# Places in SBUF: weight tiles and the activations that meet them begin at multiples of 256 bytes

## The chip, the cores and the metric

The kernel runs on one core of a Trainium2 chip. The metric is the device time of one execution in microseconds (us): the median over several runs. A profiled execution gives one further time and the trace that the views below are taken from.

## What is computed

One layer of a streaming encoder, on 512 tokens of 1024 channels, all in float32. Cut to what matters:

```python
h = rms_norm(x, norm_mix_pre)
(a_q, a_k, a_v, f_q, f_k, f_v, f_g, c_u, s_x, s_b, s_c) = split(h @ w_in)
ya = diff_attention(a_q, a_k, a_v, lam)            # 4 heads, rms norm behind it
yf = forgetting_attention(f_q, f_k, f_v, log_f)    # 8 heads
yc = silu(layer_norm(dwconv31(glu(c_u))))
ys = s_b * dwconv3(s_c * s_x)
gates = sigmoid(h @ w_gate + b_gate)               # 4 x 1024 columns
mixed = sum_n(gates[n] * (y[n] @ w_branch[n])) @ w_out
x = x + rms_norm(mixed, norm_mix_post)
hx = rms_norm(x, norm_x_pre); m = rms_norm(mem, norm_mem)
x = x + rms_norm(cross_attention(hx @ w_xq, m @ w_xkv) @ w_xo, norm_x_post)
hf = rms_norm(x, norm_ffn_pre)
u_g, u_v = split(dwconv3(hf @ w_up))               # 2 x 2816 columns
x = x + rms_norm((silu(u_g) * u_v) @ w_down, norm_ffn_post)
```

## The kernel before

**Three products for one.** Every large matrix product is made of three matmuls in the type float32r. Each operand is held as a high part and a low part (what the high part leaves over): hth and htl for the activations, wh and wl for the weights, and so on. `mm3` (L195) issues high x high, high x low and low x high into the same PSUM bank, through `matmul` (L187), so nearly all matmuls have L188 as their line. A matmul has two operands in SBUF: the **stationary** one, 128 columns, loaded into TensorE ahead of it, and the **moving** one, up to 512 columns, streamed through. `channel_major` (L201) makes an output with channels on partitions: for each of 8 blocks of 128 input channels a 128 x 128 piece of the weights is stationary and 512 tokens of ht move; that is 24 matmuls for one weight block. In `v_jobs`, `mix_out_jobs`, `vx_jobs`, `cross_out_jobs` and `down_jobs` (L1240) it is the other way round: 128 tokens of the activation are stationary and 512 columns of the weights move.

**Weights.** All weights come in 180 blocks of 512 KB (four of 520 KB). `load_raw` (L128) issues the DMA from SP into one of two raw tiles wr; `split_weights` (L136) makes wh by a copy on ScalarE (L148) and wl by a subtraction on VectorE (L149). wh and wl have four buffers each, which come round by turns (the pool gives out a buffer that has been released). A tile of them has WB = 1040 float32 elements, 4160 bytes to a partition; most blocks fill 4096 of these, the block of the forget values (`vf_jobs`, 2 x 520 columns) all. `run_blocks` (L161) goes through one list of jobs (`all_jobs`, L1283): it fetches two blocks ahead, then runs a block's body.

**Order.** A scheduler of the language orders each engine's instructions at build time, but for the first stretch of the kernel, which is written out by hand (`keep`, L264). Small tasks (attention steps, convolution taps, norms) are put between the blocks by `Background` (L44) with estimated costs. In order of time: the first columns of w_in with the norm of x (to 35 us), the convolution and short-convolution columns, the gates and branches in turn with the two attentions (to some 590 us), the output projection, the cross attention (640 to 740 us), the up-projection (44 blocks, to 973 us) and the down-projection (22 blocks, to the end). The up-projection has two outputs of 128 x 512 for each of its 22 pairs of blocks; the down-projection adds up in all eight PSUM banks at once: for a block, each of four token tiles has two halves of 512 columns with three matmuls each, and two banks of one tag stand for a token tile, so that six matmuls in a row name the same PSUM tag.

**Where tiles stand.** Pools give tiles their places in SBUF, in the order in which tiles are first asked for, one behind another. The pool "g" (L86) lies at the low end and holds ident, ht, the mask, wr, wh, wl and small tiles; the pools m2, res, work and ffn follow it upward; the pools m1, xm, mix and xp are taken from the upper end. All pieces within a tile that matmuls read begin at multiples of 256 bytes from the tile's start, but in the block of the forget values, where half of them begin 32 further. These are the places (bytes from the start of a partition) of the built programs, taken modulo 256:

| tile | met by | before | after |
|---|---|---|---|
| hth, htl (h, hx, hf) | w, wa | 160, 160 | 0, 0 |
| wh, wl: buffers 1 to 4, in the order of their first use | ht, y8, mix, mt, ox, act | 32, 224, 160, 96 | 0, 0, 0, 0 |
| wa (first columns, high and low) | ht | 160 | 160 |
| y8 (branch outputs) | w | 224 | 0 |
| mixh, mixl | w | 96 | 0 |
| mth, mtl; later oxh, oxl | w | 96 | 0 |
| kx / xq | each other | 96 / 224 | 0 / 128 |
| vx / pth, ptl of the cross attention | each other | 224 / 96 | 0 / 0 |
| acth, actl | w | 224 | 0 |
| qk; v and pth, ptl of the attentions | themselves; each other | 160; 32 | 160; 32 |
| wr (raw weights; DMA, ScalarE, VectorE) | no matmul | 160, 224 | 128, 192 |

wh and wl of one block always stand at the same place modulo 256.

Of the kernel before, what the change touches and what calls it, by code (L numbers as in the profile page):

```python
# [16 lines left out]
F32 = mybir.dt.float32  # L17
F32R = mybir.dt.float32r
# [6 lines left out]
P = 128  # L25
S = 512
D = 1024
NT = S // P
NK = D // P
# [4 lines left out]
NF = DFF // P  # L34
EPS = 1e-6
WB = 2 * 520
BIG = -float(2.0 ** 100)
LAMBDA_INIT = 0.8 - 0.6 * math.exp(-0.3 * 0)

# [41 lines left out]
def hybrid_layer(ctx: ExitStack, tc: tile.TileContext, a: dict, out: bass.AP):  # L81
# [4 lines left out]
    gp = ctx.enter_context(tc.tile_pool(name="g", bufs=1))  # L86
# [7 lines left out]
    def bank(tag=None):  # L94
        if tag is None:
            turn_of.n += 1
            tag = "av" if turn_of.shared and turn_of.n % 2 else "mm"
        return psum.tile([P, 512], F32, tag=tag, name=f"ps_{tag}", bufs=2)
# [14 lines left out]
    G.memset(nhalf, -0.5)  # L113


    def split(ps, hi, lo, scale=None):

        if scale is None:
            A.copy(hi, ps)  # L119
            V.tensor_tensor(lo, ps, hi.bitcast(F32), ALU.subtract)  # L120
        else:
            A.activation(hi, ps, AF.Copy if isinstance(scale, float) else AF.Identity, scale=scale)
            V.scalar_tensor_tensor(lo, ps, scale, hi.bitcast(F32), ALU.mult, ALU.subtract)
# [4 lines left out]
    def load_raw(src, shape, order=same):  # L128

        n = int(math.prod(shape[1:]))  # L130
        raw = gp.tile([P, WB], F32, tag="wr", name="wr", bufs=2)
        t = raw[:, :n]
# [3 lines left out]
    def split_weights(raw, shape, low=V, order=same):  # L136

        n = int(math.prod(shape[1:]))
        hi = gp.tile([P, WB], F32R, tag="wh", name="wh", bufs=4)
        lo = gp.tile([P, WB], F32R, tag="wl", name="wl", bufs=4)  # L140
        names = "k c" if len(shape) == 3 else "c"
        form = f"p ({names}) -> p {names}"

        def view(t):
            t = t[:, :n]
            return t.rearrange(form, k=shape[1]) if len(shape) == 3 else t

        order(A.copy(hi[:, :n], raw[:, :n]))  # L148
        low.tensor_tensor(lo[:, :n], raw[:, :n], hi[:, :n].bitcast(F32), ALU.subtract)  # L149
        return view(hi), view(lo)  # L150

    def load_weights(src, shape, low=V, order=same):
        return split_weights(*load_raw(src, shape), low, order)
# [77 lines left out]
    def to_channels(y_t, act, t):  # L231

        sl = slice(t * P, (t + 1) * P)
        for half in range(2):
            ps = bank("tr")
            ks = slice(half * 4, half * 4 + 4)
            for k in range(4):
                transpose(ps[:, k * P:(k + 1) * P], y_t[:, (half * 4 + k) * P:(half * 4 + k + 1) * P])
            split(ps.rearrange("p (k c) -> p k c", k=4), act[0][:, ks, sl], act[1][:, ks, sl])

    def new_ht():
        return (gp.tile([P, NK, S], F32R, tag="hth", name="hth"),
                gp.tile([P, NK, S], F32R, tag="htl", name="htl"))


    ht = new_ht()
    tc.swap_default_side()
    m1 = tc.tile_pool(name="m1", bufs=1)
# [10 lines left out]
    G.memset(mask_a, 0.0)  # L259
    G.memset(mask_a[0:HD, S - HD:S], BIG)  # L260

# [38 lines left out]
    for i, plan in enumerate(plans):  # L300
        r_t = m1p.tile([P, P], F32, tag="fbias" if i == 2 else "ck", name=f"rows{i}", bufs=2)
        n = 0
# [92 lines left out]
    for p in range(3):  # L395
        first_half(1, p, w_a[1], glu)
    casts = []
    w_g = [split_weights(*raw, V, lambda ins: casts.append(keep(ins))) for raw in raw_g]


# [9 lines left out]
    def pc(name, j=0, n=1):  # L410
        i, base = where[name]
        return par[i][:, base + j:base + j + n]
# [7 lines left out]
            par.append(t)  # L420

    def scaled(name, n, factor):
        t = gp.tile([P, n], F32, name=f"s_{name}")
        V.tensor_scalar(t, pc(name, 0, n), factor, None, ALU.mult)
        return t

# [2 lines left out]
    def finish_init():  # L429
        to_columns()  # L430
        half["glu"] = scaled("b_glu", 8, 0.5)
        half["gate"] = scaled("b_gate", 32, 0.5)
        half["ln_g"] = scaled("ln_g", 4, 0.5)
        half["ln_b"] = scaled("ln_b", 4, 0.5)
        half["dn"] = scaled("dn", 1, 1.0 - LAMBDA_INIT)

    lam = gp.tile([P, 1], F32, name="lam")
    bfg = gp.tile([P, 8], F32, name="bfg")


    def y8(dtype=F32R):
# [275 lines left out]


    crows = dram.tile([8, S], F32, name="crows")
    cq = gp.tile([P, NT, 8], F32, name="cq")  # L720

    def vf_jobs(dst):

# [79 lines left out]
    def f_task(p, qk, v):  # L803
# [10 lines left out]
        for step in range(6):  # L814
# [17 lines left out]
            if step < 4:  # L832
# [3 lines left out]
                for j in range(2):  # L836
# [5 lines left out]
                    G.affine_select(out=bias[:, w - P:w], in_=bias[:, w - P:w], pattern=[[-1, P]],  # L842
                                    compare_op=ALU.is_ge, fill=BIG, base=0, channel_multiplier=1)
                    ps = bank("sc")
# [94 lines left out]
    ns = SimpleNamespace()  # L939

    def new_pool(name, right):
        if right:
            tc.swap_default_side()
        pool = tc.tile_pool(name=name, bufs=1, reuse_waits="tile")
        handle = pool.__enter__()
        if right:
            tc.swap_default_side()
        return pool, handle

    def close(pool):  # L950
        pool.__exit__(None, None, None)

    def stage(tag, name):
        return ns.xm.tile([P, D], F32, tag=tag, name=name)

    def open_last_branch():
        close(m1)
        ns.xm_, ns.xm = new_pool("xm", True)
        ns.mt = (ns.xm.tile([P, NK, MEM], F32R, tag="mth", name="mth"),
                 ns.xm.tile([P, NK, MEM], F32R, tag="mtl", name="mtl"))  # L960
        ns.kx = (ns.xm.tile([P, 4, MEM], F32R, name="kxh"), ns.xm.tile([P, 4, MEM], F32R, name="kxl"))
        ns.gain = stage("s0", "g_mem")
        G.dma_start(ns.gain, a["norm_mem"][0].partition_broadcast(P))
        bg.add(mem_task(), "mem")
        ns.mix_, ns.mixp = new_pool("mix", True)
        ns.mix = (ns.mixp.tile([P, NK, S], F32R, name="mixh"), ns.mixp.tile([P, NK, S], F32R, name="mixl"))

    def mem_task():
        for t in range(2):
            m_t = stage("s1", "m_t")  # L970
            G.dma_start(m_t, mem_d[t * P:(t + 1) * P, :])
            y_t = normed(ns.xm, m_t, [ns.gain], stage("s2", "mn"))
            yield 1.3, 8.0
            to_channels(y_t, ns.mt, t)
            yield 1.2, 0.0
# [25 lines left out]
    def last_branch_jobs():  # L1001
        yield then(open_last_branch)
        yield from gate_blocks(1, "f", lambda m: split(acc[m], ns.mix[0][:, m], ns.mix[1][:, m], 0.5))
# [26 lines left out]
    def open_mix_out():  # L1030
        close(m2)
        ns.res_, resp = new_pool("res", False)
        ns.out = [resp.tile([P, D], F32, name=f"res{t}") for t in range(NT)]
        ns.work_, ns.work = new_pool("work", False)
        ns.vx = (ns.work.tile([P, 2, BR], F32R, name="vxh"), ns.work.tile([P, 2, BR], F32R, name="vxl"))
        ns.post, ns.pre = stage("s0", "g_post"), stage("s1", "g_pre")
        G.dma_start(ns.post, a["norm_mix_post"][0].partition_broadcast(P))
        G.dma_start(ns.pre, a["norm_x_pre"][0].partition_broadcast(P))
        ns.hx = new_ht()
        ns.x = {}  # L1040
        load_x(0)
        load_x(1)
# [116 lines left out]
    def open_cross_out():  # L1159
        ns.ox = (ns.xm.tile([P, 4, S], F32R, tag="mth", name="oxh"),  # L1160
                 ns.xm.tile([P, 4, S], F32R, tag="mtl", name="oxl"))
        ns.post, ns.pre = stage("s0", "g_post2"), stage("s1", "g_pre2")
        G.dma_start(ns.post, a["norm_x_post"][0].partition_broadcast(P))
        G.dma_start(ns.pre, a["norm_ffn_pre"][0].partition_broadcast(P))
        ns.hf = new_ht()
# [162 lines left out]
```

## Time and profile before

| | |
|---|---|
| median of 3 runs | 1102.9 us (1102.79 to 1107.03) |
| the profiled execution's own time | 1103.45 us |
| its span, first to last instruction | 1101.7 us |
| TensorE (PE) busy | 1088.4 us, 5445 matmuls |
| VectorE (DVE), ScalarE (ACT) busy | 695.2 and 463.4 us |
| mean granted TensorE clock | 0.998 of full speed |
| DMA | 109.29 MB, 99 GB/s |

The page of the profile gives busy times by engine, then the chain that ended last (from the last instruction back, at each step to what released it), then groups of equal instructions: line, engine, operation, output<-inputs, shapes, count, then busy us and mean ns of one, then the idle time before them with what ended it. PE stands for matmuls, PEld for the loads of stationary operands. Matmuls are pipelined, and the printed time of one contains the wait behind its predecessor: 5445 matmuls of mostly 390 ns would be far more than the span. Their starts follow each other at 230 ns or so, and it is the starts that carry time. The chain's own view in order of time merges neighbours of one group: start, duration, engine, output, line, count.

### The profile page before, as it was taken

Reading aid. Unit: us, or ns where it says so; the run is one execution under the profiler, and the core shown is the slowest. Engines: PE = TensorE matmul, PEld = TensorE weight load, DVE = VectorE, ACT = ScalarE, POOL = GpSimd, SP = SyncE. Lnnn points to the kernel's source line nnn. Section 1 sums busy time; section 2 is a strip of 40 time slices with the busy share of each in tenths; the row PEclk is TensorE's granted clock in tenths of the full one; section 3 lists DMA queues with packets and bytes.
Section 4 is the critical chain, followed back from the end, with each engine's and each line's share of the span. In section 5 each row is a group of like instructions: output and inputs, shape, how many; then the busy total and the mean of one; then the engine's idle time right before and its main releaser. Section 6 shows DMA issues by size and latency. Waiting matters only on the chain.

```text
span 1101.7 us, 14173 instructions
## 1 busy us (share of the span) xinstructions
PE 1088.4 (99%) x5445; PEld 912.7 (83%) x5445; DVE 695.2 (63%) x1128; ACT 463.4 (42%) x783; POOL 100.6 (9%) x186
## 2 busy tenths in 40 slices
PE   8999999999999999999999999999999999999997
PEld 7888888888888988888888899788888888888886
DVE  6899986466666367757563486668666666642224
ACT  5322222467464365554432455545444444431111
POOL 4000001000101033323010110120000000000001
PEclk9999999999999999999999999999999999999999
DMA  6433433332122243333252263133333333323222
GB/s 198 115 96 82 96 96 98 94 96 77 58 86 69 79 114 96 96 96 115 86 180 94 80 188 101 56 97 115 96 96 96 96 96 96 95 96 96 96 77 77
DMA packets 145849, 109.29 MB, mean 99 GB/s; under 512 B 3648, under 2 KB 133293, under 8 KB 145782
## 3 DMA queue, kind: packets, MB, share of 16 engines
q1 hardware_dynamic: 143221, 99.85, 30.4%
q0 software_dynamic: 2560, 8.54, 2.7%
q8 instruction: 43, 0.70, 0.3%
q14 instruction: 25, 0.20, 0.1%
HBM read 106.27 MB, written 2.11 MB: 98 GB/s over the span
## 4 chain that ended last, share of the span: by engine, by line
PE 94%; DMA 2%; DVE 1%; ACT 1%; issue 1%; POOL 0%; POOLq 0%; DVEq 0%; SPq 0%; ACTq 0%
PE ps_mm L188 49%; PE ps_av L188 30%; PE ps_sc L188 8%; PE ps_tr L192 3%; PE ps_tr L188 3%; DVE wl L149 1%; DMA wr<-in_w_xo 1%; ACT wh L148 1%; PE ps_mm L369 1%; PE ps_av L369 1%; DMA wr<-in_w_xkv 0%; DMA wr<-in_w_xq 0%; DMA xs<-in_x 0%; POOL st_r L218 0%; ACT hth L119 0%
## 5 line engine op out<-in xcount | busy, mean ns | idle before, releaser
L149 DVE TENSOR_TENSOR wl<-wr,wh 128x1024 fp32r<-128x1024 f32 (+1 forms) x180 | 222.1, 1235 | 216.0 <-ACT wh L148 215.3
L148 ACT CAST wh<-wr 128x1024 fp32r<-128x1024 f32 (+1 forms) x180 | 188.5, 1049 | 340.5 <-PE ps_mm L188 127.6
L188 PE MATMUL ps_mm<-hth,wh 128*128 128x512 f32 (+1 forms) x608 | 233.7, 385 | 0.4 <-ACT hth L119 0.2
L188 PE MATMUL ps_mm<-hth,wl 128*128 128x512 f32 (+1 forms) x608 | 232.5, 382 | 0.0
L188 PE MATMUL ps_mm<-htl,wh 128*128 128x512 f32 (+1 forms) x608 | 232.3, 382 | 0.2 <-DVE htl L120 0.2
L188 PEld LDWEIGHTS ps_mm<-hth,wh 128*128 128x128 f32 x608 | 114.4, 188 | 22.2 <-ACT hth L119 0.5
L188 PEld LDWEIGHTS ps_mm<-hth,wl 128*128 128x128 f32 x608 | 114.3, 188 | 22.3
L188 PEld LDWEIGHTS ps_mm<-htl,wh 128*128 128x128 f32 x608 | 114.4, 188 | 21.6 <-DVE htl L120 0.5
L188 PE MATMUL ps_av<-hth,wh 128*128 128x512 f32 (+1 forms) x336 | 127.2, 379 | 0.2
L188 PE MATMUL ps_av<-htl,wh 128*128 128x512 f32 (+1 forms) x336 | 126.9, 378 | 0.0
L188 PE MATMUL ps_av<-hth,wl 128*128 128x512 f32 (+1 forms) x336 | 126.9, 378 | 0.0
L517 DVE SCALAR_TENSOR_TENSOR y<-y,par,y 128x499 f32<-128x499 f32 (+28 forms) x120 | 82.4, 731 | 0.2
L188 PEld LDWEIGHTS ps_av<-hth,wh 128*128 128x128 f32 x336 | 63.2, 188 | 13.1 <-DVE e L864 0.5
L188 PEld LDWEIGHTS ps_av<-hth,wl 128*128 128x128 f32 x336 | 63.2, 188 | 12.6
L188 PEld LDWEIGHTS ps_av<-htl,wh 128*128 128x128 f32 x336 | 63.2, 188 | 12.4
L188 PE MATMUL ps_mm<-y,wh 128*128 128x512 f32 x192 | 61.5, 397 | 0.0
L215 POOL TENSOR_SCALAR st_m<-pm,pm 128x1 f32<-128x1 f32 x12 | 4.6, 387 | 483.5 <-ACT junk L1269 357.5
L188 PEld LDWEIGHTS ps_mm<-y,wh 128*128 128x128 f32 x192 | 35.4, 188 | 7.3
L188 PE MATMUL ps_mm<-y,wl 128*128 128x512 f32 x96 | 37.9, 395 | 0.0
L119 ACT CAST acth<-c 128x512 fp32r<-128x512 f32 x22 | 13.6, 620 | 55.8 <-DVE c L1216 55.8
L119 ACT CAST pth<-ps_tr 128x512 fp32r<-128x512 f32 (+3 forms) x56 | 23.6, 450 | 28.8 <-PE ps_tr L192 26.1
L120 DVE TENSOR_TENSOR ptl<-ps_tr,pth 128x512 fp32r<-128x512 f32 (+3 forms) x56 | 28.0, 513 | 10.6 <-ACT pth L119 10.3
(373 smaller groups left out, 1893.8 us busy)
## 6 DMA issues: line engine op xcount, KB each, us to landing
wr<-in_w_up SPq DMA_DIRECT2D x44, 512.0 KB
wr<-in_w_in SPq DMA_DIRECT2D x38, 512.0 KB
wr<-in_w_gate SPq DMA_DIRECT2D x32, 512.0 KB
wr<-in_w_down SPq DMA_DIRECT2D x22, 512.0 KB
wr<-in_w_branch SPq DMA_DIRECT2D x16, 512.0 KB
wr<-in_w_out SPq DMA_DIRECT2D x8, 512.0 KB
wr<-in_w_xkv SPq DMA_DIRECT2D x8, 512.0 KB
wr<-in_w_in SPq DMA_DIRECT2D x4, 520.0 KB
```

Source lines behind the costliest of these rows:

```text
L119: A.copy(hi, ps)
L120: V.tensor_tensor(lo, ps, hi.bitcast(F32), ALU.subtract)
L148: order(A.copy(hi[:, :n], raw[:, :n]))
L149: low.tensor_tensor(lo[:, :n], raw[:, :n], hi[:, :n].bitcast(F32), ALU.subtract)
L188: PE.matmul(ps, lhs, rhs, start=start, stop=stop)
L192: PE.transpose(ps, x, ident[:n, :n])
L215: G.tensor_scalar(m, parts[0], parts[1], EPS, ALU.add, ALU.add)
L369: keep(PE.matmul(banks[c][:, :S // 2], w[p == 1][:, k, c * P:(c + 1) * P], ht[p == 2][:, i * 4 + k, :S // 2], start=(i, p, k) == (0, 0, 0) ...
L517: V.scalar_tensor_tensor(dst[:, s:], src[:, :S - s], pc("conv_dw", k * 4 + j), dst[:, s:], ALU.mult, ALU.add)
```

## The change

No instruction is added or taken away; tiles are taken in another order, and some space is left between them.

- `small` and `ht_tiles` take the small tiles lam, bfg and s_dn, and then the first hth and htl, ahead of the others, so that ht begins at a multiple of LINE = 256. `new_ht` (L241) hands out these two first.
- The eight weight tiles are taken at once, wh and wl in turn. Behind the first stand s_b_gate, s_b_glu and s_ln_g (176 bytes, rounded up by the pool to 192); behind each of the next six a gap of 192 bytes; behind the last cq, s_ln_b and a gap of 160. Each tile has a tag of its own; `weights_tile` counts the uses and goes round the four in a fixed order.
- A gap of 96 bytes in the pool xm, behind kx, sets mt, kx, mix and what follows in the upper pools.
- All else moves by what lies below it (the table above).

```diff
+LINE = 256
...
+    small = {n: gp.tile([P, k], F32, name=n) for n, k in (("lam", 1), ("bfg", 8), ("s_dn", 1))}
+    ht_tiles = [gp.tile([P, NK, S], F32R, tag=n, name=n) for n in ("hth", "htl")]
+    w_tiles, w_used = {}, {"wh": 0, "wl": 0}
+
+    def space(pool, name, n):
+
+        if n:
+            pool.tile([P, n // 4], F32, name=name)
+
+    for i in range(8):
+        n = ("wh", "wl")[i % 2]
+        w_tiles[n, i // 2] = gp.tile([P, WB], F32R, tag=f"{n}{i // 2}", name=n)
+        if i == 0:
+            small.update((n, gp.tile([P, k], F32, name=n)) for n, k in (("s_b_gate", 32), ("s_b_glu", 8), ("s_ln_g", 4)))
+        elif i < 7:
+            space(gp, f"gap{i}", -4 * WB % LINE)
+    small.update((n, gp.tile([P, k], F32, name=n)) for n, k in (("cq", NT * 8), ("s_ln_b", 4)))
+    space(gp, "gap7", 160)
+
+    def weights_tile(kind):
+
+        i = w_used[kind]
+        w_used[kind] += 1
+        return w_tiles.pop((kind, i), None) or gp.tile([P, WB], F32R, tag=f"{kind}{i % 4}", name=kind)
...
-        hi = gp.tile([P, WB], F32R, tag="wh", name="wh", bufs=4)
-        lo = gp.tile([P, WB], F32R, tag="wl", name="wl", bufs=4)
+        hi, lo = weights_tile("wh"), weights_tile("wl")
...
     def new_ht():
+        if ht_tiles:
+            return ht_tiles.pop(0), ht_tiles.pop(0)
...
-        t = gp.tile([P, n], F32, name=f"s_{name}")
+        t = small[f"s_{name}"]
...
-    lam = gp.tile([P, 1], F32, name="lam")
-    bfg = gp.tile([P, 8], F32, name="bfg")
+    lam, bfg = small["lam"], small["bfg"]
...
-    cq = gp.tile([P, NT, 8], F32, name="cq")
+    cq = small["cq"].rearrange("p (t h) -> p t h", t=NT)
...
+        space(ns.xm, "gap8", 96)
```

## The prediction

> **What bounds the kernel.** I read the page first, then the chain of work that ended last, then the starts of TensorE's instructions one by one.
>
> ```profile
> span 1101.7 us, 14173 instructions
> ...
> PE 1088.4 (99%) x5445; PEld 912.7 (83%) x5445; DVE 695.2 (63%) x1128; ACT 463.4 (42%) x783; POOL 100.6 (9%) x186
> ...
> PE 94%; DMA 2%; DVE 1%; ACT 1%; issue 1%; POOL 0%; POOLq 0%; DVEq 0%; SPq 0%; ACTq 0%
> PE ps_mm L188 49%; PE ps_av L188 30%; PE ps_sc L188 8%; PE ps_tr L192 3%; PE ps_tr L188 3%; DVE wl L149 1%; DMA wr<-in_w_xo 1%; ACT wh L148 1%; PE ps_mm L369 1%; PE ps_av L369 1%; DMA wr<-in_w_xkv 0%; DMA wr<-in_w_xq 0%; DMA xs<-in_x 0%; POOL st_r L218 0%; ACT hth L119 0%
> ...
> L148 ACT CAST wh<-wr 128x1024 fp32r<-128x1024 f32 (+1 forms) x180 | 188.5, 1049 | 340.5 <-PE ps_mm L188 127.6
> ```
>
> The chain is 94% TensorE, nearly all of it line 188. The last line says who waits for whom: ScalarE, which makes the high parts of the weights, sits idle because TensorE hasn't yet given a buffer back. So the time is the number of matmuls times the distance between their starts. (The printed 385 ns of a matmul is no price: matmuls overlap. I take start to start.) 3871 of the 5445 rows are 512 columns wide; their starts take up 899.3 us, 232.3 ns each. Long waits are few: behind the first 20 us only six, all between 641 and 740 us, hold TensorE by over 0.3 us beyond a matmul's own time, 4.3 us together.
>
> **A natural experiment in the trace of before.** The up-projection is the cleanest stretch: blocks of 24 equal matmuls, no waits. The chain there, columns start us, us, what:
>
> ```profile
> 851.53 5.50 PE ps_mm L188 x24
> 857.03 5.60 PE ps_av L188 x24
> 862.62 5.46 PE ps_mm L188 x24
> 868.09 5.58 PE ps_av L188 x24
> ```
>
> Same instruction, same shape, same granted clock of 1.00, yet four durations that come round every four blocks: that is the rotation of the four wh/wl buffers. A tile of 4160 bytes shifts the next one's place by 64 modulo 256. The table of places ahead of this section gives the rest: the moving hth and htl stand at 160, and the four stationary blocks above stand at 96, 224, 160 and 32. I call **distance** the place of the stationary operand less that of the moving one, modulo 256: here 192, 64, 0 and 128. Distance 0 is the shortest block. I laid the program's 5440 matmuls beside the trace's rows, in order, and grouped the 512-wide ones (intervals over 250 ns left out of the means):
>
> - distance 0: 932, mean 228.6 ns; in the steady part of a block 226.7
> - distance 64: 1068, mean 233.2 (steady 231 and 236 in turn, or 233)
> - distance 128: 804, mean 232.4 (a pattern between 228 and 241)
> - distance 192: 1066, mean 229.6 (226, 229, 232 in turn)
>
> Is it the distance, or the buffer? The down-projection has the sides exchanged: w moves, act (at 224) is stationary, so that another buffer, the one at 224, is at distance 0. The chain there:
>
> ```profile
> 989.99 1.40 PE ps_mm L188 x6
> 991.38 1.37 PE ps_av L188 x6
> 992.75 1.36 PE ps_sc L188 x6
> 994.11 1.36 PE ps_tr L188 x6
> 995.47 1.40 PE ps_mm L188 x6
> 996.87 1.40 PE ps_av L188 x6
> 998.27 1.40 PE ps_sc L188 x6
> 999.67 1.40 PE ps_tr L188 x6
> ```
>
> The first four rows are the buffer at 224: after one row of settling 1.36 us for 6, or 226.7 ns. The next four are the buffer at 160, distance 64: 1.40, or 233.3. In the up-projection these two were the other way round. So the distance decides, not the buffer, the PSUM bank or the time.
>
> The Trainium skill ("SBUF — State Buffer", sections "SBUF: two separate sides" and "A bandwidth-pool intuition that's wrong") says that TensorE's SBUF ports never wait on anyone and that LDWEIGHTS has a second, independent read port; by it places cost nothing, the sum is 0 and the time stays 1102.9. The trace doesn't agree: 5.46 against 5.60 us for the same 24 matmuls.
>
> **The change, part by part.** It adds no instruction on any engine: matmuls, casts, subtractions and DMAs are the same in number and shape. The order differs in two short stretches (the first gate blocks, 157 to 169 us, where six and seven of TensorE's matmuls change places with their neighbours; and 540 to 562 us, where transposes of the memory tokens and ScalarE's casts beside them move by a block). TensorE has no wait there that the profile shows, and weights are ready 8 us and more ahead (below), so I put nothing down for it, at most 0.5 us either way.
>
> *512-wide matmuls.* After the change hth, htl, mt, mix, ox, y8 and act begin at 0, and so do all eight weight tiles: every pair with weights is at distance 0. Slices inside these tiles begin at whole multiples of 256, but for the forget-value block, whose rows of 520 columns set half of its slices 32 further, as they do now. Two bounds. If each class falls to the mean that distance 0 has now, 1068 x 4.6 + 804 x 3.8 + 1066 x 0.9 ns = 4.9 + 3.1 + 1.0 = 9.0 us. If each falls to the undisturbed distance-0 block, 5.455 / 24 = 227.3 ns, 1068 x 5.9 + 804 x 5.1 + 1066 x 2.3 + 932 x 1.3 = 6.3 + 4.1 + 2.4 + 1.2 = 14.0 us. The difference is settling: after a disturbance some eight matmuls run mostly between 228 and 236 before 226.7 is reached, about 30 ns in all. Runs of equal distance now start 370 times: 202 by a change of distance (those go), 103 by another shape, 65 after a wait (both stay). So 3871 x 226.7 = 877.5, plus 168 x 0.03 = 5.0, plus the 5.6 us of waits on such matmuls: 888.1, that is 11.2 less than 899.3, near the middle of the bounds. I take **11.3 us**.
>
> *256-wide matmuls.* Here distance 0 is the worst: means 119.1 (0), 115.1 (64), 118.9 (128), 117.1 (192). 180 and 132 go from 64 and 192 to 0: 180 x 4.0 + 132 x 2.0 = 1.0 us lost. The wa tiles stay at 160 while hth goes to 0: a distance of 160 for some 100 rows that were at 0; the few rows at odd multiples of 32 read 117 to 118, so it is 0.1 us gained, nothing. kx against xq stays at 128; qk and v against pt keep their places; vx against pt goes from 128 to 0, which the means price alike. **1.0 us lost.**
>
> *What is late next.* The time between a wl tile's completion and its first use is 14.5 us in the up-projection and 14 in the down-projection, over two blocks; DVE, the busiest helper, has 99.0 of 103 us from 37 to 140 us, yet its wl tiles are 5 to 18 us early there. A TensorE faster by 1% uses 0.06 us of that per block. The cover is thin at one place, where 256-wide blocks eat weights faster than they come:
>
> ```profile
> 636.50 4.81 DMA wr<-in_w_xkv
> 641.34 1.05 ACT wh L148
> 642.41 1.24 DVE wl L149
> 643.66 4.59 DMA wr<-in_w_xq
> ```
>
> From 634 to 658 us weight tiles are used 0.7 to 2 us after they are made, and five of TensorE's six long waits lie between 641 and 726 us. The 144 wide matmuls of vx and of the cross output stand in or near it: up to 144 x 3 = 0.4 us of their gain is given back. It stays in the range.
>
> *Places of everything else.* DVE's 1235 ns and ScalarE's 1049 ns for a weight tile show no trend with the buffer (undisturbed medians 1224 to 1226 and 1048 to 1052 over all places). Nothing is put down.
>
> Sum: 1.0 - 11.3 = -10.3 us against the profiled execution, 1103.45, whose span is 1101.7: 1093.1. It lies 0.5 above the median of the runs shown, 1102.9, so I say **1092.5** for the median. The case's own range is 1088 (14.0, no loss) to 1096 (9.0 less 1.0, 0.4 and 0.5).
>
> **Rivals.**
> - *A place of 0 is itself better.* All weight pairs of before begin at 32 modulo 64; none has both ends at a multiple of 64, so this is not shown. Between 256 and 512 columns at distance 0 the steady interval rises by 226.7 - 120.0 = 106.7, so 512 columns alone are 213.3 and 13.3 ns are extra; the best steady 256-wide rows (113.3, distance 64) have 6.7. With 6.7 on each wide matmul another 3871 x 6.7 = 25.8 us go: about 1067. Against it: in the forget-value products w, as the moving side, stands at 0, 64, 128 or 192 in half of the rows, and these read 115 to 123, no better than their neighbours.
> - *The two reads collide at the start of a line* (slower). At a multiple of 256 both operands begin at the same point of a line in every matmul. The 256-wide rows are worst at equal places, so equal places can be the clash. If the wide ones went to the longest interval that recurs now, 241 ns, then 3871 x 8.7 = +34 us: 1137. It decides once the wide mean passes 232.6. Against it: at 32, 96, 160 and 224 alike, wide matmuls at distance 0 aren't slower than others.
> - *Nothing comes of it*: the places don't matter as I think, or another engine's pace takes up the gain in the casts. About 1103. Against it: the two exchanged rotations, and the 14 us of lead.
>
> **Chances.** Forecast 0.75, place-0 bonus 0.10, nothing 0.08, collision 0.07. To hold 8 in 10 the range goes some way to the bonus and to nothing: 1080 to 1099. About 0.5%, 5.5 us, is what a measurement of this kernel can tell from no change. Faster by more (under 1097.4): 0.75 + 0.10 = 0.85; within: 0.08; slower: 0.07.
>
> **What would show it.** In the changed profile every 24-block of the up-projection reads 5.44 to 5.46, with no cycle of four, and the 22 blocks of the down-projection likewise (1.36 per 6); the stretch of 256-wide work around 640 to 700 us is no shorter. Wrong if blocks still alternate (places aren't the cause), if all read the same but not 5.45 (the place counts beside the distance), or if waits on wh or wl appear in the chain.

## The result and the profile after

The changed kernel takes 1091.46 us (median of 4 runs, 1091.4 to 1091.97) against 1103.18 for the kernel before (1102.79 to 1107.03). By the medians that is 11.7 us less; 1092.5 was forecast. The ratio of the two sets of runs is 0.9883, 95% interval 0.9867 to 0.99; this ratio, here and below, isn't the quotient of the medians, which would be 0.9894.

From the page of the changed kernel (line 188 of before is L214 here, 148 is L174):

```profile
span 1090.2 us, 14173 instructions
...
PE 1077.4 (99%) x5445; PEld 913.5 (84%) x5445; DVE 694.5 (64%) x1128; ACT 463.9 (43%) x783; POOL 99.8 (9%) x186
...
PE 95%; DMA 1%; DVE 1%; ACT 1%; issue 1%; POOL 0%; POOLq 0%; DVEq 0%; SPq 0%; ACTq 0%
...
L174 ACT CAST wh<-wr 128x1024 fp32r<-128x1024 f32 (+1 forms) x180 | 188.5, 1049 | 328.0 <-PE ps_mm L214 126.8
```

All counts are as before; TensorE lost 11.0 us of busy time and no other engine as much as 1. It is the bound as before (95% of the chain, 94% before), and ScalarE still waits for TensorE to give buffers back. The chain in the up-projection, in order of time (start us, us, what):

```profile
839.08 5.44 PE ps_av L214 x24
844.52 5.44 PE ps_mm L214 x24
849.96 5.44 PE ps_av L214 x24
```

The cycle of 5.50, 5.60, 5.46 and 5.58 is gone: every block that the chain shows whole takes what the best of the four took, less its settling (24 x 226.67 = 5.440). The same view in the down-projection, where the sides are exchanged:

```profile
975.08 1.36 PE ps_mm L214 x6
976.44 1.36 PE ps_av L214 x6
977.80 1.36 PE ps_sc L214 x6
```

Where the 11.5 us of the span came from, by the starts of the same matmuls in both traces:

| stretch (us in the kernel before) | before | after | difference |
|---|---|---|---|
| first columns, to 37 | 37.1 | 37.6 | +0.5 |
| 37 to 351: columns, convolutions, gates, first attention | 314.0 | 310.2 | -3.8 |
| 351 to 643: forget values, second attention, last gates, output projection | 292.0 | 289.3 | -2.7 |
| 643 to 760: cross attention, first four up blocks | 117.0 | 117.7 | +0.7 |
| 760 to 976: up-projection | 215.6 | 211.7 | -3.9 |
| 976 to the end: down-projection and output | 125.9 | 123.7 | -2.2 |

The wide matmuls' starts went from 899.3 to 887.0 us, the 256-wide ones' from 127.2 to 128.2.

### The profile page after: what moved, and what is told of

Read it like the earlier page. It is cut to its first block, busy times and chain, and to the rows that moved or that the text cites. A ratio compares the mean times of both kernels' runs of the same rounds, so it can differ in the third digit from the quotient of the medians.

```text
span 1090.2 us, 14173 instructions
## 1 busy us (share of the span) xinstructions
PE 1077.4 (99%) x5445; PEld 913.5 (84%) x5445; DVE 694.5 (64%) x1128; ACT 463.9 (43%) x783; POOL 99.8 (9%) x186
## 4 chain that ended last, share of the span: by engine, by line
PE 95%; DMA 1%; DVE 1%; ACT 1%; issue 1%; POOL 0%; POOLq 0%; DVEq 0%; SPq 0%; ACTq 0%
PE ps_mm L214 50%; PE ps_av L214 30%; PE ps_sc L214 8%; PE ps_tr L218 3%; PE ps_tr L214 3%; DMA wr<-in_w_xo 1%; PE ps_mm L397 1%; PE ps_av L397 1%; DVE wl L175 1%; DMA wr<-in_w_xq 0%; ACT wh L174 0%; DMA xs<-in_x 0%; POOL st_r L244 0%; PE ps_tr L381 0%; ACT hth L146 0%
## 5 line engine op out<-in xcount | busy, mean ns | idle before, releaser
L175 DVE TENSOR_TENSOR wl<-wr,wh 128x1024 fp32r<-128x1024 f32 (+1 forms) x180 | 221.6, 1232 | 206.7 <-ACT wh L174 206.2
L174 ACT CAST wh<-wr 128x1024 fp32r<-128x1024 f32 (+1 forms) x180 | 188.5, 1049 | 328.0 <-PE ps_mm L214 126.8
L214 PE MATMUL ps_mm<-hth,wh 128*128 128x512 f32 (+1 forms) x608 | 232.6, 383 | 0.5 <-ACT wh L174 0.3
L214 PE MATMUL ps_mm<-hth,wl 128*128 128x512 f32 (+1 forms) x608 | 231.3, 380 | 0.0
L214 PE MATMUL ps_mm<-htl,wh 128*128 128x512 f32 (+1 forms) x608 | 231.1, 380 | 0.1
L214 PEld LDWEIGHTS ps_mm<-hth,wh 128*128 128x128 f32 x608 | 114.5, 188 | 21.4 <-ACT hth L146 0.5
L214 PEld LDWEIGHTS ps_mm<-hth,wl 128*128 128x128 f32 x608 | 114.4, 188 | 21.1
L214 PEld LDWEIGHTS ps_mm<-htl,wh 128*128 128x128 f32 x608 | 114.4, 188 | 20.4 <-DVE htl L147 0.5
L214 PE MATMUL ps_av<-hth,wh 128*128 128x512 f32 (+1 forms) x336 | 126.0, 375 | 0.6 <-ACT wh L174 0.5
L214 PE MATMUL ps_av<-htl,wh 128*128 128x512 f32 (+1 forms) x336 | 125.8, 375 | 0.0
L214 PE MATMUL ps_av<-hth,wl 128*128 128x512 f32 (+1 forms) x336 | 125.7, 374 | 0.0
L214 PEld LDWEIGHTS ps_av<-hth,wh 128*128 128x128 f32 x336 | 63.1, 188 | 12.3 <-ACT wh L174 0.7
L214 PEld LDWEIGHTS ps_av<-hth,wl 128*128 128x128 f32 x336 | 63.3, 188 | 11.3
L214 PEld LDWEIGHTS ps_av<-htl,wh 128*128 128x128 f32 x336 | 63.3, 188 | 11.2
L214 PE MATMUL ps_mm<-y,wh 128*128 128x512 f32 x192 | 61.0, 394 | 0.1
L241 POOL TENSOR_SCALAR st_m<-pm,pm 128x1 f32<-128x1 f32 x12 | 4.7, 389 | 476.9 <-ACT junk L1297 351.6
L214 PEld LDWEIGHTS ps_mm<-y,wh 128*128 128x128 f32 x192 | 35.3, 188 | 7.3 <-ACT ge L908 0.6
L214 PE MATMUL ps_mm<-y,wl 128*128 128x512 f32 x96 | 37.7, 393 | 0.0
```

The costliest lines, as they stand in the source:

```text
L214: PE.matmul(ps, lhs, rhs, start=start, stop=stop)
L241: G.tensor_scalar(m, parts[0], parts[1], EPS, ALU.add, ALU.add)
```

## The experiments

The theory on record: the distance between the two operands of a float32r matmul, modulo 256 bytes, sets the interval between starts. The rivals: a place at a multiple of 256 (or 64) is itself what pays; the weight tiles' common place pays, whatever the other operand does; the pattern needs other engines' accesses; or nothing in TensorE changed at all. In all versions of the whole kernel below, the instructions of every engine stand in the same order as in the changed kernel, so that places alone differ.

### Everything at 160 instead of 0

```diff
-    small = {n: gp.tile([P, k], F32, name=n) for n, k in (("lam", 1), ("bfg", 8), ("s_dn", 1))}
+    small = {}
...
+        elif i == 1:
+            small.update((n, gp.tile([P, k], F32, name=n)) for n, k in (("lam", 8), ("bfg", 8), ("s_dn", 8)))
+            space(gp, "gap1", 96)
...
-        space(ns.xm, "gap8", 96)
+        space(ns.xm, "gap8", 192)
```

The small tiles ahead of ht go into a gap, and all behind moves down by 96 bytes.

> The changed kernel with everything moved so that ht, the weight tiles, y8, mix, mt, ox and act begin at 160 modulo 256 instead of 0 (no such tile begins at a multiple of 256 or of 64 any more); every pair with weights stays at distance 0, and every engine's instructions stand in the same order. Theory (the distance between the two operands decides): 1091.5 us, within 1 us of the changed kernel; 24-blocks of the up-projection at 5.44. Rival (a start at a multiple of 256, or of 64, is itself what pays): back to about 1103, blocks at 5.5 to 5.6.

Measured: 1094.04 us (1090.6 to 1094.51), a ratio of 0.9893 (0.9867 to 0.9919) to the kernel before on the same chip; the changed kernel's 0.9883 lies inside. In the chain, blocks of the up-projection:

```profile
841.12 5.44 PE ps_av L217 x24
846.56 5.44 PE ps_mm L217 x24
```

No tile that meets the weights begins at a multiple of 64 here, and every block still takes 5.44. The wide matmuls' starts sum to 887.1 us, against 887.0 in the changed kernel: the place by itself is worth nothing. The median misses the expected 1091.5 by 2.5 us, more than the 1 us allowed. One of the four runs took 1090.6, and in the profiled one (1094.08) the second attention waited longer for its rows of cumulated gates. The chain there, with transfers that the changed kernel's chain doesn't name:

```profile
391.01 3.32 DMA crows<-e
...
394.63 4.20 DMA ck<-crows
```

The one transfer that writes crows took 3.3 us from issue to landing there and 2.1 in the changed kernel, and the attention's stretch was 128.5 us long against 126.5. So in the profiled execution the difference comes in with that transfer, not with the matmuls' own pace; why it took longer there isn't settled, and the two other runs near 1094 left no trace.

### The weight tiles alone 64 bytes on

```diff
+    space(gp, "lead", 64)
     for i in range(8):
         n = ("wh", "wl")[i % 2]
...
-    space(gp, "gap7", 160)
+    space(gp, "gap7", 96)
```

> The changed kernel with the eight weight tiles alone moved on by 64 bytes; all operands still begin at multiples of 64, and the instructions stand in the same order. 2880 wide matmuls go to distance 64, 960 to distance 192, 576 of the 256-wide ones to 64. Theory: 2880 x 5.7 + 960 x 2.4 - 576 x 4.3 ns = 16.4 + 2.3 - 2.5 = 16.2 us more than the changed kernel, 1107.7, slower than the kernel before; up-projection blocks all at 5.60, down-projection rows of six at 1.37 to 1.38. Rival (starts at multiples of 64 are enough): 1091.5.

Measured: 1106.48 us (1105.73 to 1110.51), 1.0016 (1.0001 to 1.0031) of the kernel before: all of the gain is gone, though ht, the weights, y8, mix, mt, ox and act all begin at multiples of 64 and the eight weight tiles share a place. The chain, first in the up-projection (distance 64), then in the down-projection (192):

```profile
843.46 5.60 PE ps_mm L215 x24
849.06 5.60 PE ps_av L215 x24
```

```profile
1005.34 1.37 PE ps_mm L215 x6
```

Both as expected. The span was 14.9 us above the changed kernel's, 16.2 were expected: wide matmuls' starts 17.2 (expected 18.7), 256-wide ones -1.9 (expected -2.5). By class, distance 64 costs what was expected (233.2 ns against 227.5 in the changed kernel, 5.7 more), but 192 costs 1.6 ns (229.1) and not 2.4, which is 0.8 us over 960 matmuls; waits on wide matmuls were also some 0.4 us shorter. Two rivals fall here: starts at multiples of 64 aren't enough, and a common place of the weight tiles isn't either. The order of the instructions isn't the cause either, since it is the changed kernel's.

### Matmuls alone: a sweep of the distance

The kernel leaves the layer out; it is two tiles and one loop:

```python
def group(name, x, w, size, xb, wb, width, count=48):
    ps = psum.tile([P, 512], F32, tag=f"b{banks[0] % 8}", name=name)
    banks[0] += 1
    for n in range(count):
        x0, w0 = xb // size + (n % 8) * 512, wb // size + (n % 8) * P
        keep(PE.matmul(ps[:, :width], w[:, w0:w0 + P], x[:, x0:x0 + width], start=n == 0, stop=n == count - 1))
    keep(V.tensor_copy(junk[:, banks[0] % 8:banks[0] % 8 + 1], ps[:, 0:1]))
```

> Matmuls alone, none of the layer is computed (the output is zeros and a few sums): groups of 48 matmuls with operands in two tiles that begin at a multiple of 256, the stationary one shifted by d bytes (r512d.., r256d.., r384d.. in float32r, h512d.. in bfloat16), both shifted by b (r512b..), or the moving one alone (r512m..). No other engine reads or writes SBUF meanwhile but for one small copy per group. Theory: start to start 226.7 ns at d = 0 whatever b is; 233.3, 232.4 and 229.2 at d = 64, 128, 192; the moving one shifted by 64 reads like d = 192; 256 columns 120, 113.5, 118, 117. Rival (the pattern needs the other engines' reads and writes): all groups of 512 columns read the same.

Measured: 620.1 us. The chain gives each group of 48 one line; 10.88 is 226.67 each, 11.20 is 233.3. First the stationary operand moved on by d, then both by b, then the moving one alone by 64 and 128:

```profile
37.77 10.88 PE r512d0z L80 x48
48.65 10.89 PE r512d16z L80 x48
59.54 11.19 PE r512d32z L80 x48
...
81.93 11.19 PE r512d64z L80 x48
...
126.68 11.20 PE r512d128z L80 x48
...
171.31 10.99 PE r512d192z L80 x48
...
204.70 10.91 PE r512d240z L80 x48
215.61 11.16 PE r512d4z L80 x48
226.77 11.07 PE r512d8z L80 x48
...
271.33 11.47 PE r512b4z L80 x48
282.81 11.21 PE r512b8z L80 x48
294.01 11.04 PE r512b16z L80 x48
305.06 10.93 PE r512b32z L80 x48
...
348.73 10.91 PE r512b160z L80 x48
...
381.47 10.99 PE r512m64z L80 x48
392.46 11.14 PE r512m128z L80 x48
```

But for one small copy per group no other engine is at work here, so the pattern is TensorE's own and lies between its two operands; the rival that needs other engines' accesses falls. Moving one operand on is nearly the same as moving the other back: m64 settles at 228.9 ns like d192, m192 at 233.3 like d64, but m128 at 232.1 where d128 has 233.3. The shortest interval, 226.67 ns, is reached at d = 0, 16 and 240, but not at 4 and 8 (232.5 and 230.7); d = 192 comes next (228.9), and most other distances settle at 233.3. Two things the theory missed. At 256 columns it gave 120, 113.5, 118 and 117 ns for the distances 0, 64, 128 and 192, and the groups settle at 120.0, 117.8, 118.8 and 117.8. And with 512 columns, distance 0 alone isn't all. If both operands start 4, 8 or 16 bytes past a multiple of 32, the last 24 intervals are 239.2, 233.4 and 230.0 ns; from 32 on the common place doesn't matter. The pools here give places in steps of 32, so the kernel never met this. At 384 columns, distances 0, 32 and 192 settle at 173.3 ns and the others at 174.5 to 176.7.

In bfloat16 the eight distances read alike: the matmuls that the trace holds, 376 of 384, follow each other at 215.8 ns. The Trainium skill ("TensorE: Matmul & The Clock Gate", section "Wait — 56ns, not 53.3ns?") gives 215.7 ns for 512 columns on a warm array; the bfloat16 groups agree, and the float32r groups stay 11 to 23 ns above it.

### One part of the change alone

As in the version at 160, but with

```diff
-    space(gp, "gap7", 160)
+    space(gp, "gap7", 224)
...
-        space(ns.xm, "gap8", 96)
+        space(ns.xm, "gap8", 0)
```

so that ht and the weights share 160 while y8 and act stand at 224, and mix, mt and ox at 96.

> One part of the change alone: ht and the eight weight tiles share a place (160, as ht has it in the kernel before), but y8 and act stand at 224 and mix, mt and ox at 96, as before the change. Instructions stand in the same order as in the changed kernel. 528 wide matmuls are at distance 64 (w_down) and 720 at 192. Theory: 528 x 6.6 + 720 x 2.1 - 96 x 4 ns = 3.5 + 1.5 - 0.4 = 4.6 us more than the changed kernel beside it; up-projection blocks 5.44, down-projection rows of six 1.40. Rival (it is the weight tiles' common place that pays, not how it stands to the other operand): the time of the changed kernel.

The changed kernel beside it on the same chip:

> The changed kernel itself, beside the one-part kernel on the same chip, as the scale for it: 0.989 of the kernel before by every theory.

Measured: 1095.83 us (1095.13 to 1096.18) against 1091.12 (1090.89 to 1092.09): 4.7 us more, where 4.6 were expected; ratios to the kernel before 0.9921 (0.9906 to 0.9936) and 0.9881 (0.9862 to 0.9899). The chain has the up-projection as in the changed kernel and the down-projection as in the worst quarter of before:

```profile
844.77 5.44 PE ps_mm L217 x24
```

```profile
992.45 1.40 PE ps_mm L217 x6
```

So of the 14.4 us between the medians on that chip (1105.54 before) 9.7 go with bringing the weight tiles to ht's place, and 4.7 with bringing the other activations there too. The 9.7 is the less sure, since the runs of before spread there from 1101.87 to 1106.51: by the starts of the wide matmuls in the traces the parts are 7.6 (899.3 to 891.7) and 4.9 us (891.7 to 886.8).

### Matmuls alone: modulus, widths, narrow operands

The same loop with other arguments, and with `m` columns of the stationary operand or a shift of every second one.

> Matmuls alone again, nothing of the layer is computed. r512d256z to r512d448z: distances beyond 256. Theory (places count modulo 256): 226.7, 233.3, 233.3, 228.9, as at 0, 64, 128, 192. r256: 256 columns at all distances in steps of 16; 120 at 0 and 117.5 to 120 elsewhere. c64 and c32: a stationary operand of 64 and 32 columns with 512 moving ones. Theory (the stationary operand's read takes its time out of the moving stream): the 13.3 ns above 213.3 shrink with the columns, 220.0 and 216.7 at distance 0, and the distance matters less. Rival (a fixed cost for each matmul): 226.7 at distance 0 for all. alt64, alt128, alt192: every second stationary operand is shifted; if it is the next operand's load under the running matmul that collides, short and long intervals take turns.

Measured: 369.5 us. In the chain:

```profile
47.86 10.88 PE r512d256z L80 x48
58.74 11.20 PE r512d320z L80 x48
69.94 11.16 PE r512d384z L80 x48
81.10 10.99 PE r512d448z L80 x48
...
92.09 5.76 PE r256d0z L80 x48
...
114.95 5.45 PE r256d64z L80 x48
...
160.43 5.44 PE r256d192z L80 x48
...
182.83 11.04 PE c64d0z L80 x48
193.87 11.17 PE c64d64z L80 x48
...
227.09 11.12 PE c32d0z L80 x48
```

256 is the modulus: 256, 320, 384 and 448 read like 0, 64, 128 and 192. At 256 columns the order is turned round: 113.3 ns at distances 64 and 192 and 120.0 at 0 (in the first sweep both 64 and 192 had settled at 117.8, so one distance has more than one steady pattern, and the 113.3 isn't sure to be met). Narrower stationary operands failed both theories: with 64 columns 230.0 ns at distance 0 and with 32 columns 231.7, neither 220.0 and 216.7 nor 226.7. So it isn't simply the bytes of the stationary operand that come out of the moving stream. Shifting every second stationary operand by 64 or 128 gave 232 on average, near the shifted value, and by 192 it gave 230.0, in patterns over several matmuls, and no plain taking of turns; whether it is the next operand's load that collides stays open.

## Why the prediction was right

- **The distance, not the buffer**: right. The versions at 160 and with the weights 64 bytes on differ in places alone and read 5.44 and 5.60; the sweeps show it without the layer.
- **Wide matmuls, 11.3 us**: 12.3. The mis-sized term is the settling, 5.0 us on record. With the interval over 250 ns left out, the mean in the changed kernel is 227.52, so settling cost 3797 x 0.85 ns = 3.2 us. Waits on wide matmuls cost 6.3 us over 226.7 (5.6 on record). 877.4 + 3.2 + 6.3 = 886.9, the measured 887.0. A long run still loses some 30 ns, but many of the 172 runs end, by another shape or a wait, before they have settled (99 have fewer than six matmuls and lose 4 ns each on average): 19 ns a run on average.
- **256-wide matmuls, 1.0 us lost**: 127.2 to 128.2, right in kind, in its size partly by luck. With intervals capped at 200 ns, to leave the waits out, the loss is 1.4 us (122.95 to 124.38): the rows from distance 64 lost 4.4 ns each and those from 192 lost 2.3, 1.1 us together, and the rows from 128, which the means priced alike, some 0.2. Waits on such matmuls were 0.4 us shorter.
- **The thinly covered stretch gives up to 0.4 us back**: not seen. The 144 wide matmuls of vx and of the cross output kept their gain, 0.4 us (33.9 to 33.5), and TensorE's six long waits are no longer than before (4.3 and 4.0 us). That the stretch from 643 to 760 us took 0.7 us more has other reasons: its 256-wide intervals lost 0.7, and a wait for weights that lay just ahead of it in the kernel before lies inside it now, while its wide matmuls gained 0.5.
- **Order and casts cost nothing**: right. Over each of the two stretches with another order the same matmuls get 0.3 us further ahead (1.4 to 1.7 and 3.8 to 4.1), with no new wait. ScalarE's 1049 and VectorE's 1232 ns for a weight tile are as before (1049, 1235), with wr at 128 and 192 instead of 160 and 224.
- **The rival that a place of 0 is itself better**: refuted, 5.44 at 160 as at 0, and 226.67 ns at all common places from 32 on. **The rival that equal places collide**: refuted for 512 columns; for 256 columns equal places are the worst, as the trace of before had it.
- **No change, 1102.9 us**: the Trainium skill ("SBUF — State Buffer", section "SBUF: two separate sides") says that TensorE's SBUF ports never wait on anyone. The prediction took from it that places cost nothing; the sweep speaks against that for float32r, 10.88 against 11.20 us for 48 matmuls, and for it in bfloat16. Whether TensorE's reads ever wait for another engine's isn't tested here.
- **Two slips in the working**, of no weight: 1102.9 less 14.0 is 1088.9, not 1088, and with 1.0 us lost elsewhere the time is no shorter from a wide mean of 232.1 ns on, not 232.6.

What stays open is the mechanism inside TensorE: why 0 is best for 512 columns and 64 or 192 for 256, and what the narrow stationary operands wait for.

## What to carry to other kernels

In a kernel that TensorE bounds with float32r matmuls of 512 columns, let all operands that meet start at the same place modulo 256 bytes (and at a multiple of 32). Here four rotating buffers of 4160 bytes spread over four distances, and that cost 1 to 3% on three quarters of the wide matmuls. To find it, take the interval between the starts of equal matmuls, block by block: a duration that comes round with the number of buffers points at their places, as it did here. Whether it pays for other widths has to be measured; for 256 columns the best distance was another one, for 448 distances 0 and 64 read alike (202.5 and 202.3 ns), and in bfloat16 with 512 columns there was nothing to gain.

## What the runs showed that was not expected

- Common places that aren't multiples of 32 bytes cost time at distance 0 too: 239.2 ns at 4, longer than at any distance tried, 233.4 at 8, 230.0 at 16, against 226.67.
- At distance 0 the intervals at 256, 320, 384 and 512 columns (120.0, 146.7, 173.3 and 226.7 ns) grow by 26.67 ns for every 64 columns. So the 13.3 ns that the prediction found on top of 512 columns is there at all four widths, and whether distance 0 is best or worst depends on what other distances add to it (up to 7.8 ns at 512) or take from it (up to 6.7 at 256). At 448 columns this fails: 202.5 ns in place of 200.0.
- Float32r matmuls of 128 and of 192 columns, each with a new stationary operand of 128 columns, both follow at 111.7 ns, at distance 0 and 64 alike; 320 columns follow at 146.7 at both. So between 128 and 192 the number of moving columns doesn't set the pace; that the load of the stationary operand does is likely, but no run here shows it.
- A stationary operand of 32 or 64 columns isn't faster to pass than one of 128 (231.7 and 230.0 against 226.67 ns at distance 0).
